# Modulation sums moved from TensorE products to VectorE inside three feed-forwards, with partition sums by ones and a reordered first stage

## The chip, the cores and the metric

The kernel runs on one core of one Trainium2 chip. The metric is the device time of one execution in microseconds (us). A core has a matrix engine (TensorE, PE in the profile; its weight loads are listed as PEld), three other compute engines that the profile calls DVE (VectorE), ACT (ScalarE) and POOL (GpSimd), and SP (SyncE), whose queue issues nearly all transfers here. Each engine works through its own queue in order; semaphores tie the queues together.

## What is computed

A two-layer block over 256 latent and 256 context tokens of width 1024, followed by a second two-layer block, all in float32. What matters here is the adaptive modulation of the first block:

```python
def adaln_modulation(cond, w_ada, b_ada):
    return jnp.split(jax.nn.silu(cond) @ w_ada + b_ada, N_MOD, axis=-1)   # N_MOD = 9

for layer in range(2):
    mods_lat = adaln_modulation(c, ada_w[layer], ada_b[layer])        # one vector of 1024
    mods_ctx = adaln_modulation(c_ctx, ada_w[layer], ada_b[layer])    # one vector of 1024
    x   = ffn_sublayer(x,   *mods_lat[0:3], ...)     # shift, scale, gate
    ctx = ffn_sublayer(ctx, *mods_ctx[0:3], ...)
    ... mixer with mods[3:6], then a feed-forward of the latent (and in layer 0 the context) with mods[6:9]
```

`ada_w[layer]` is 1024 x 9216, 36 MB; it is multiplied by only two vectors. In the code it is cut into 18 groups per layer (36 in all) of 512 output columns, 2 MB each. Two groups make one of the nine vectors, so groups 0 to 5 give shift, scale and gate of the first feed-forward, 6 to 11 those of the mixer and 12 to 17 those of the second feed-forward. The other operation that matters is the feed-forward, `(silu(x @ gate) * (x @ up)) @ down` with an inner width of 2816 = 22 chunks of 128.

## The kernel before

The program is written in the order of the model, and a planner in the language's framework lays out each engine's queue from that order and its own cost figures; what is emitted early can be put between instructions emitted later, and the queues are then fixed.

**Products.** Weights come as float32 into a raw tile (`wraw`, two buffers), ScalarE rounds them to `whi` (line 78) and VectorE subtracts to get `wlo` (line 81), four buffers each, one for half a chunk. `mm3` (lines 110 to 114) then makes three matmuls per block: high by high, high by low, low by high.

**Feed-forward.** `ffn` (line 1680) calls `gate_up`, which goes over 22 chunks `c`: load 1 MB, split it, and make 48 matmuls of 512 columns (gate and up, 8 row blocks, 3 matmuls each) into two PSUM banks; then ScalarE takes the silu into `h` (line 430) and VectorE multiplies (line 431). After it `rows_out` (line 434) multiplies by the down weights, 22 features of 24 matmuls.

**Modulation.** `ada_group(l, g)` (line 204) loads two tiles `fraw` of 1 MB (two buffers), makes 8 float32 products with the 32-column tile `sil` (silu of the two conditions) as the stationary operand, each on its own 32 columns of the array (line 215), copies the result to `far` (ScalarE, line 218), turns it by four transposes (line 221), sums the four quarters into `fm` (VectorE, line 223) and adds the bias. Each float32 product appears as two matmul instructions in the trace.

**Where the 36 groups stand.** Layer 0: groups 0 to 3 in `first_rows` (line 304), 4 to 9 between the chunks of the first feed-forward (every third chunk), 10 to 17 in the even mixer. Layer 1: 0 to 5 in the even mixer and its scan (`ada_next`), 6 to 9 in the third feed-forward, 10 to 17 ahead of the odd mixer's attention. In the even mixer VectorE also makes two convolutions: five taps in `conv5`, and 31 taps on four blocks in `conv31` (line 949), which the planner uses as filler from 493 us on.

**First stage.** `first_rows` computes groups 0 and 2, loads and turns the four token tiles `x`, computes group 1, modulates rows 0 to 3, loads gate and up chunk 0, computes group 3, loads chunk 1, and modulates rows 4 to 7. `gate_up` begins after all that.

Of the kernel before, what the change touches and what calls it, by code (L numbers as in the profile page):

```python
# [9 lines left out]
F32 = mybir.dt.float32  # L10
# [3 lines left out]
ALU = mybir.AluOpType  # L14
# [39 lines left out]
class Net:  # L54
    def __init__(self, tc, I, out, stop=None, dbg=None):
        self.tc, self.nc, self.I, self.out = tc, tc.nc, I, out
        self.stop, self.dbg = stop, dbg
        self.xtag = ("xtt", 2)
        self.mark = lambda label: None
        self.ahead = []  # L60
        self.pins = []
        self.norm = {}


# [138 lines left out]

    def ada_group(self, l, g):

        self.mark(f"ada{l}")
        nc = self.nc
        mod, half = divmod(g, 2)
        ps = self.pt(role="ada")
        w = self.I["ada_w"][l].rearrange("(k p) n -> p k n", p=128)  # L210
        for u in range(2):
            raw = self.fp.tile([128, 4, 512], F32, name="fraw", tag="fraw", bufs=self.FB)
            nc.sync.dma_start(raw, w[:, 4 * u:4 * u + 4, g * 512:(g + 1) * 512])
# [3 lines left out]
        r = self.fp.tile([128, 512], F32, name="far", tag="far", bufs=1)  # L217
        nc.scalar.copy(r, ps)
        p2 = self.pt([128, 4, 128], "ada")
        for j in range(4):  # L220
            nc.tensor.transpose(p2[:, j, :], r[:, 128 * j:128 * (j + 1)], self.ident)
        f = self.fm[l][:, mod, 4 * half:4 * half + 4, :]
        nc.vector.tensor_reduce(f, p2.rearrange("p j (q r) -> p j r q", q=4)[:, :, 0:2, :], axis=AX.X, op=ALU.add)
        b = self.adab[l][:, mod * 8 + 4 * half: mod * 8 + 4 * half + 4]
        nc.vector.tensor_add(f, f, b[:, :, None].to_broadcast([128, 4, 2]))

    def ada_next(self, n=1):

        for _ in range(min(n, len(self.fill))):
            self.ada_group(*self.fill.pop(0))  # L230
        self.mark("e_x")

# [71 lines left out]
    def first_rows(self, src, xh, xl):  # L304

        nc = self.nc
        xT = self.lp.tile([128, KC, 512], F32, name="xT")
        self.ada_group(0, 0)
        self.ada_group(0, 2)
        self.mark("xt0")  # L310
        for t in range(4):
            x = self.lp.tile([128, D], F32, name="x", tag="x", bufs=4)
            nc.sync.dma_start(x, src[t])
# [6 lines left out]
        self.ada_group(0, 1)  # L320
        self.mark("xt0")
        sc = self.cp.tile([128, KC, 2], F32, name="msc", tag="msc", bufs=2)
        bi = self.fm[0][:, 0]

        def modulate(k):
            if k % 4 == 0:
                nc.vector.tensor_scalar(sc[:, k:k + 4], self.fm[0][:, 1, k:k + 4], 1.0, None, op0=ALU.add)
            t = self.lp.tile([128, 512], F32, name="xtt", tag="xtt", bufs=2)
# [4 lines left out]
            self.lo(xl[:, k], t, xh[:, k])  # L333

        for k in range(4):
            modulate(k)
        self.ahead.append(self.gu_chunk(self.I["ffn_w_gu"][0, 0], 0))
        self.ada_group(0, 3)
        self.ahead.append(self.gu_chunk(self.I["ffn_w_gu"][0, 0], 1))
        self.mark("xt0")  # L340
        for k in range(4, KC):
            modulate(k)

    def xt_tiles(self, pool, T):
# [61 lines left out]

    def gate_up(self, wgu, xh, xl, T, h, fill=(), halves=()):
        nc = self.nc
        todo = []
        fill = list(fill)  # L410
        for c in range(NF):
            if fill and c >= 2 and c % 3 == 0:
                self.ada_group(*fill.pop(0))
                self.mark("gu")
            pieces = self.ahead.pop(0) if self.ahead else self.gu_chunk(wgu, c)
            ps = [self.pt([128, T]) for _ in range(2)]
            todo.append((c, pieces, ps))

            if c == 0 and T == 512:
# [9 lines left out]
            for cc, _, pp in todo:  # L429
                nc.scalar.activation(h(cc), pp[0], AF.Silu)  # L430
                nc.vector.tensor_mul(h(cc), h(cc), pp[1])
            todo = []

    def rows_out(self, w, nf, T, operand, done, keep=3, spare=None, banks=(0, 2, 4, 6), aside={}):
# [18 lines left out]
        for u in range(nf // 2):  # L453
# [3 lines left out]
            for q in range(2):  # L457
# [14 lines left out]
                if i < 0:  # L472
                    for t in range(nt):
                        prod(t, f)
                if f in aside:
                    aside[f]()
        for t in range(nt):
# [22 lines left out]
    def even(self, xh, xl):  # L500
# [148 lines left out]
        for h in range(4):  # L649
# [6 lines left out]
            tokmajor(c, khat[:, :, h, :])  # L656
            if h % 2:
                self.ada_next()
        rk = gd.tile([128, 16], F32, name="rk")
# [65 lines left out]
        for b2 in range(2):  # L725
            pv, pg = unit(2064 + 256 * b2), unit(2576 + 256 * b2)
            for j in range(2):
# [8 lines left out]
                pads.append(pad)  # L736
                self.ada_next()

# [3 lines left out]
        for h in range(4):  # L742
# [4 lines left out]
            sumsq(qT[:, h, :], h, pss)  # L747
            if h % 2:
                self.ada_next()
        rq = gd.tile([128, 16], F32, name="rq")  # L750
# [12 lines left out]
        for h in range(4):  # L763
# [6 lines left out]
            nc.sync.dma_start(kvd[:, :, 1, h, :].rearrange("t p c -> p t c"), vt)  # L770
            if h % 2:
                self.ada_next()

        self.mark("e_z")

        for h in range(4):
# [5 lines left out]
            nc.sync.dma_start(szd[h], c)  # L782
            if h % 2:
                self.ada_next()

# [3 lines left out]
    def even_scan(self, E):  # L789
# [187 lines left out]
        both(step(0, 3, False, False), step(1, 2, False, False))  # L977
        self.ada_next(20)
        merge(2)
# [10 lines left out]

    def odd(self, xh, xl, oh, ol, fill, aside):
        nc, tc, I = self.nc, self.tc, self.I
# [91 lines left out]
        self.roles(mm=[2, 3], tp=[0], sc=[4, 5], po=[1], ada=[6, 7])  # L1084
        for g in fill:
            self.ada_group(*g)
        self.mark("o_att")
        for h in range(8):
# [415 lines left out]
    def run(self):  # L1504
        nc, tc, I = self.nc, self.tc, self.I
        with ExitStack() as ctx:
# [24 lines left out]
            with tc.tile_pool(name="lp", bufs=1, reuse_waits="tile") as self.lp:  # L1531
                self.first_rows(raw, *xt)
            later()
            xt = self.ffn(0, 0, 512, xt, raw, src(0), lambda x: feed(0, (3, 4), 0, x), ada(0, 4, 10))
            if self.stop == "ffn00":
                return dump(0)
            with tc.tile_pool(name="yo", bufs=1, reuse_waits="tile") as self.yo:
                self.roles(mm=[2, 3], tp=[0, 1], ch=[4, 5], ada=[6], pss=[7])
                with tc.tile_pool(name="gd", bufs=1, reuse_waits="tile") as self.gd:
                    with tc.tile_pool(name="ip", bufs=1, reuse_waits="tile") as self.ip:  # L1540
                        self.fill = ada(0, 10, 18) + ada(1, 0, 6)
                        E = self.even(*xt)
# [10 lines left out]
            if self.stop == "mix0":  # L1553
                return dump(1)
            xt = self.ffn(0, 1, 512, xt, src(1), src(2), lambda x: feed(1, (0, 1), 2, x), cuts=((256, 512), (0, 256)))
            if self.stop == "x0c":
                return dump(2, 2)
            xt = self.ffn(1, 0, 512, xt, src(2), src(3), lambda x: feed(1, (3, 4), 3, x), ada(1, 6, 10))
            if self.stop == "x1a":
# [5 lines left out]
            with tc.tile_pool(name="oo", bufs=1, reuse_waits="tile") as oo:  # L1565
                ot = oo.tile([128, KC, 256], F32R, name="oh"), oo.tile([128, KC, 256], F32R, name="ol")
                with tc.tile_pool(name="od", bufs=1, reuse_waits="tile") as self.od:
                    self.roles(mm=[2, 3, 4, 5], tp=[0, 1], sc=[4, 5], po=[7], ada=[6])
                    self.odd(*xt, *ot, ada(1, 10, 18), lambda: self.memory_rows(0, self.od, *self.mem))
                xt = self.mix_out(1, I["attn_w_out"][0], 256, lambda f: (ot[0][:, f, :], ot[1][:, f, :]),  # L1570
# [108 lines left out]

    def ffn(self, l, i, T, xt, srcs, dsts, feed, fill=(), cuts=((0, 256), (256, 512))):  # L1680

# [3 lines left out]
        with tc.tile_pool(name="gp", bufs=1, reuse_waits="tile") as self.gp, \  # L1685
# [5 lines left out]
            h = lambda c: h0[:, c, :] if c < n0 else h1[:, c - n0, :]  # L1691
            self.roles(mm=[2, 3, 4, 5], tp=[0, 1], ada=[6, 7])
            self.mark(f"gu{l}{i}")
            self.gate_up(I["ffn_w_gu"][l, i], xt[0], xt[1], T, h, fill, cuts)
            self.mark(f"dn{l}{i}")
# [49 lines left out]
```

## Time and profile before

| | |
|---|---|
| median of 3 runs | 2547.15 us (2544.28 to 2547.5) |
| the profiled execution's own time | 2545.8 us |
| its span in the trace | 2544.0 us |
| mean granted TensorE clock | 0.992 of full speed |
| busy: PE, PEld | 2480.4, 2020.9 us |
| busy: DVE, ACT, POOL | 1417.3, 1053.4, 9.1 us |
| transfers | 395.78 MB, 156 GB/s in the mean |

The busy time of PE is modelled (a matmul's row lasts longer than the distance to the next one), so the rows below are mostly read by start times. A row of the timeline gives start, duration, engine, line, operation, output and inputs; in brackets, where shown, the idle time of the engine before it and what ended it.

### The profile page before, as it was taken

The page shows a single profiled execution, that of the slowest core. Times are in us where ns is not written, and L with a number is a line of the kernel's source. Part 1 is how long each engine was busy: PE and PEld are TensorE (multiplying, and loading weights), DVE is VectorE, ACT ScalarE, POOL GpSimd, SP SyncE. Part 2 cuts the span into 40 slices and gives each one's busy share as a digit, 9 for nine tenths or more (in the row PEclk, how much of TensorE's full clock was granted, in tenths as well). Part 3 has the DMA queues.
Part 4 walks back from the last instruction along what each step waited for, and adds up shares of the span by engine and source line. Part 5 has one row for each costly group of instructions (what it writes and reads, how often), then busy time and mean ns, then how long its engine had stood idle before and what let it go on. Part 6 is the DMA issues. An engine that isn't in the chain of part 4 may idle for free.

```text
span 2544.0 us, 33357 instructions
## 1 busy us (share of the span) xinstructions
PE 2480.4 (97%) x13192; PEld 2020.9 (79%) x13192; DVE 1417.3 (56%) x2699; ACT 1053.4 (41%) x1766; POOL 9.1 (0%) x42
## 2 busy tenths in 40 slices
PE   6999999999999999999999999999999999999998
PEld 4877887767888888888788887589978878888786
DVE  3322246699887422347322357665575766657755
ACT  2222234733334222224222325654455565556544
POOL 0000000000000000000000000000000000000000
PEclk8999999999999999999999999999999999999999
DMA  8545433476626333235453335768655335453354
GB/s 283 170 138 153 145 101 132 146 212 225 226 84 198 100 100 100 100 100 185 130 161 90 114 108 171 272 188 222 195 174 179 100 128 195 168 177 116 128 170 141
DMA packets 342634, 395.78 MB, mean 156 GB/s; under 512 B 19368, under 2 KB 236749, under 8 KB 342477
## 3 DMA queue, kind: packets, MB, share of 16 engines
q1 hardware_dynamic: 342477, 393.64, 49.0%
q8 instruction: 104, 1.70, 0.3%
q14 instruction: 53, 0.43, 0.1%
HBM read 377.06 MB, written 16.55 MB: 155 GB/s over the span
## 4 chain that ended last, share of the span: by engine, by line
PE 90%; DVE 5%; DMA 3%; ACT 1%; issue 1%; SPq 0%; DVEq 0%; ACTq 0%
PE b L112 26%; PE b L114 26%; PE b L113 26%; PE b L215 2%; DMA fraw<-in_ada_w 2%; PE b L1294 1%; PE b L287 1%; DVE wlo L81 1%; DMA wraw<-in_w_in 1%; DVE y L949 1%; PE b L1355 1%; PE b L1103 1%; PE b L1346 1%; PE b L822 0%; PE b L817 0%
## 5 line engine op out<-in xcount | busy, mean ns | idle before, releaser
L81 DVE TENSOR_TENSOR wlo<-wraw,whi 128x1024 fp32r<-128x1024 f32 (+2 forms) x499 | 600.5, 1207 | 692.2 <-ACT whi L78 691.1
L78 ACT CAST whi<-wraw 128x1024 fp32r<-128x1024 f32 (+2 forms) x499 | 514.0, 1039 | 500.5 <-PE b L113 289.9
L112 PE MATMUL b<-xh,whi 128*128 128x512 f32 (+1 forms) x1720 | 616.2, 359 | 4.0 <-ACT whi L78 2.7
L113 PE MATMUL b<-xl,whi 128*128 128x512 f32 (+1 forms) x1720 | 614.9, 358 | 0.0
L114 PE MATMUL b<-xh,wlo 128*128 128x512 f32 (+1 forms) x1720 | 612.5, 357 | 2.2 <-DVE wlo L81 2.1
L112 PEld LDWEIGHTS b<-xh,whi 128*128 128x128 f32 x1720 | 328.5, 191 | 63.8 <-issue 10.1
L113 PEld LDWEIGHTS b<-xl,whi 128*128 128x128 f32 x1720 | 328.8, 191 | 47.6 <-issue 4.2
L114 PEld LDWEIGHTS b<-xh,wlo 128*128 128x128 f32 x1720 | 328.1, 191 | 47.9 <-DVE wlo L81 3.7
L113 PE MATMUL b<-wlo,hh 128*128 128x512 f32 x652 | 254.6, 390 | 0.0
L112 PE MATMUL b<-whi,hh 128*128 128x512 f32 x652 | 254.4, 390 | 0.0
L114 PE MATMUL b<-whi,hl 128*128 128x512 f32 x652 | 254.3, 390 | 0.0
L430 ACT ACTIVATE h<-b 128x512 f32<-128x512 f32 (+1 forms) x88 | 47.9, 544 | 334.1 <-PE b L114 334.0
L112 PE MATMUL b<-whi,x 128*128 128x512 f32 (+1 forms) x448 | 172.3, 385 | 1.4 <-ACT xtt L294 1.4
L114 PE MATMUL b<-whi,x 128*128 128x512 f32 (+1 forms) x448 | 170.6, 381 | 0.0
L113 PE MATMUL b<-wlo,x 128*128 128x512 f32 (+1 forms) x448 | 170.5, 381 | 0.0
L112 PEld LDWEIGHTS b<-whi,hh 128*128 128x128 f32 x652 | 122.4, 188 | 26.2
L114 PEld LDWEIGHTS b<-whi,hl 128*128 128x128 f32 x652 | 122.4, 188 | 26.0
L113 PEld LDWEIGHTS b<-wlo,hh 128*128 128x128 f32 x652 | 122.5, 188 | 25.8
L81 DVE TENSOR_TENSOR hl<-h,hh 128x512 fp32r<-128x512 f32 (+1 forms) x81 | 50.2, 621 | 150.1 <-ACT hh L78 150.1
L78 ACT CAST hh<-h 128x512 fp32r<-128x512 f32 (+1 forms) x81 | 45.8, 567 | 195.6 <-PE b L113 189.5
L112 PEld LDWEIGHTS b<-whi,x 128*128 128x128 f32 x448 | 84.2, 188 | 18.0 <-issue 2.0
L215 PE MATMUL b<-fraw,sil 128*32 128x512 f32 x576 | 84.9, 644 | 12.8 <-DMA fraw<-in_ada_w 12.8
(477 smaller groups left out, 3232.0 us busy)
## 6 DMA issues: line engine op xcount, KB each, us to landing
wraw<-in_ffn_w_gu SPq DMA_DIRECT2D x176, 512.0 KB, 5.6
fraw<-in_ada_w SPq DMA_DIRECT2D x72, 1024.0 KB, 7.1
wraw<-in_w_in SPq DMA_DIRECT2D x64, 1024.0 KB, 5.1
wraw<-in_ffn_w_down SPq DMA_DIRECT2D x44, 1024.0 KB, 5.0
wraw<-in_even_w_in SPq DMA_DIRECT2D x12, 1024.0 KB, 6.6
wraw<-in_w_branch SPq DMA_DIRECT2D x12, 1024.0 KB, 4.9
xd<-x SPq DMA_DIRECT2D x16, 512.0 KB, 5.8
wraw<-in_w_mem_kv SPq DMA_DIRECT2D x8, 1024.0 KB
```

Of the source, the lines that this page charges most:

```text
L78: self.nc.scalar.copy(out, in_)
L81: return self.nc.vector.tensor_sub(out, in_, hi)
L112: mm(ps, ah, bh, start=start, stop=False)
L113: mm(ps, ah, bl, start=False, stop=False)
L114: mm(ps, al, bh, start=False, stop=stop)
L215: nc.tensor.matmul(ps[32 * q:32 * q + 32], self.sil[:, 4 * u + q, :], raw[:, q, :], start=(u == 0), stop=(u == 1))
L287: nc.tensor.transpose(ps[:, j, :], n[:, 128 * k:128 * (k + 1)], self.ident)
L430: nc.scalar.activation(h(cc), pp[0], AF.Silu)
L949: v.scalar_tensor_tensor(acc, pad[:, :, i:i + 256], w, acc, op0=ALU.mult, op1=ALU.add)
L1103: nc.tensor.matmul(po, vt[:, c, h // 4], pT[:, c], start=(c == 0), stop=(c == 3))
L1294: nc.tensor.matmul(ps, T[r, h // 2, 128 * t:128 * t + 128], K[r, 0:128 * (t + 1)], start=True, stop=True)
L1346: nc.tensor.transpose(p2[:, j, 128 * c:128 * c + 128], p[:, j, 128 * c:128 * c + 128], self.ident)
```

## The change

Groups 0 to 3 of layer 0 still use `ada_group`. The other 32 are made by a generator, `ada_sums`, that runs inside three feed-forwards: 12 groups (layer 0, 4 to 15) in the first, 12 (layer 0, 16 and 17; layer 1, 0 to 9) in the second, 8 (layer 1, 10 to 17) in the third. For each of the two conditions VectorE multiplies the eight 128 x 512 row blocks of a group by the condition's value on each partition and adds them up in a tile `facc`: 16 VectorE operations of 512 columns a group. Four matmuls with the first column of a constant tile of ones as the moving operand then sum over the 128 partitions, for each condition apart, and VectorE adds the bias. `gate_up` takes eight steps of the generator a chunk, `rows_out` four a feature, and the rest at its end. The even mixer, its scan and the odd mixer have no groups any more.

`first_rows` issues its loads in another order: group 0, the four token tiles, group 2, half of the weights of chunks 0 and 1, groups 1 and 3 (into six buffers of their own). It then makes the first halves of the products of chunks 0 and 1 as soon as rows 0 to 3 are modulated, groups 1 and 3 after them, and the rest of chunks 0 to 2; `gate_up` gets these three chunks ready made.

```diff
+    def ada_load(self, l, g, pool=None):
+        w = self.I["ada_w"][l].rearrange("(k p) n -> p k n", p=128)
+        out = []
+        for u in range(2):
...
+                raw = pool.tile([128, 4, 512], F32, name="araw", tag="araw", bufs=6)
+            self.nc.sync.dma_start(raw, w[:, 4 * u:4 * u + 4, g * 512:(g + 1) * 512])
...
-    def ada_next(self, n=1):
...
+    def ada_sums(self, groups):
+        def load(l, g, u):
+            raw = self.fp.tile([128, 4, 512], F32, name="fraw", tag="fraw", bufs=self.FB)
...
+        def total(l, g, s, acc):
+            if s == 0:
+                self.ada_ps = self.pt([128, 4, 2], "ada")
+            ps = self.ada_ps
+            mod, half = divmod(g, 2)
+            for j in range(4):
+                nc.tensor.matmul(ps[:, j, s:s + 1], acc[:, 128 * j:128 * (j + 1)], self.ones[:, 0:1],
+                                 start=True, stop=True)
+            if s:
...
+                nc.vector.tensor_add(self.fm[l][:, mod, 4 * half:4 * half + 4, :], ps,
+                                     b[:, :, None].to_broadcast([128, 4, 2]))
+        halves = [(l, g, u) for l, g in groups for u in range(2)]
...
+        raws = [load(*h) for h in halves[:2]]
+        acc = {}
+        for i, (l, g, u) in enumerate(halves):
+            raw = raws.pop(0)
+            for s in range(2):
+                if u == 0:
+                    acc[s] = self.lp.tile([128, 512], F32, name="facc", tag="facc", bufs=2)
+                for q in range(4):
+                    c = self.sil[:, 4 * u + q, s:s + 1]
+                    if u + q == 0:
+                        nc.vector.tensor_scalar(acc[s], raw[:, q], c, None, op0=ALU.mult)
+                    else:
+                        nc.vector.scalar_tensor_tensor(acc[s], raw[:, q], c, acc[s], op0=ALU.mult, op1=ALU.add)
+                    yield
+                if u:
+                    total(l, g, s, acc[s])
+            if i + 2 < len(halves):
+                raws.append(load(*halves[i + 2]))
...
     def first_rows(self, src, xh, xl):
-        self.ada_group(0, 0)
-        self.ada_group(0, 2)
...
+        loads = {0: self.ada_load(0, 0, lp)}
+        for t in range(4):
+            x = lp.tile([128, D], F32, name="x", tag="x", bufs=4)
+            nc.sync.dma_start(x, src[t])
+        loads[2] = self.ada_load(0, 2, lp)
...
+        raws = {(0, 0): piece(0, 0), (1, 0): piece(1, 0)}
+        self.ada_group(0, 0, loads.pop(0))
...
+        self.ada_group(0, 2, loads.pop(2))
+        loads[1] = self.ada_load(0, 1, lp)
+        loads[3] = self.ada_load(0, 3, lp)
...
         for k in range(4):
             modulate(k)
+        half(0, 0, acc[0])
+        raws[2, 0] = piece(2, 0)
+        half(1, 0, acc[1])
+        self.ada_group(0, 1, loads.pop(1))
+        self.ada_group(0, 3, loads.pop(3))
         for k in range(4, KC):
             modulate(k)
+        raws[0, 1] = piece(0, 1)
+        half(2, 0, acc[2])
+        raws[1, 1] = piece(1, 1)
+        for c in range(3):
+            if c == 1:
+                raws[2, 1] = piece(2, 1)
+            half(c, 1, acc[c])
+        return acc
...
     gate_up:   + self.ada_some(8)       # each chunk, after its load and split
     rows_out:  + self.ada_some(4)       # each of the first 17 features; at the end self.ada_some(200)
     even, even_scan:  - self.ada_next() # 14 groups
     odd:       - for g in fill: self.ada_group(*g)     # 8 groups
```

## Rows read from the trace of the kernel before

**Rows 1.** The profile page, busy time, share and instructions of each engine.

```profile
PE 2480.4 (97%) x13192; PEld 2020.9 (79%) x13192; DVE 1417.3 (56%) x2699; ACT 1053.4 (41%) x1766; POOL 9.1 (0%) x42
```

**Rows 2.** The chain that ended last: shares by engine, then by line.

```profile
PE 90%; DVE 5%; DMA 3%; ACT 1%; issue 1%; SPq 0%; DVEq 0%; ACTq 0%
PE b L112 26%; PE b L114 26%; PE b L113 26%; PE b L215 2%; DMA fraw<-in_ada_w 2%; PE b L1294 1%; PE b L287 1%; DVE wlo L81 1%; DMA wraw<-in_w_in 1%; DVE y L949 1%; PE b L1355 1%; PE b L1103 1%; PE b L1346 1%; PE b L822 0%; PE b L817 0%
```

**Rows 3.** Instructions grouped by line: count, busy us, mean ns, idle before and releasers.

```profile
L81 DVE TENSOR_TENSOR wlo<-wraw,whi 128x1024 fp32r<-128x1024 f32 (+2 forms) x499 | 600.5, 1207 | 692.2 <-ACT whi L78 691.1
...
L215 PE MATMUL b<-fraw,sil 128*32 128x512 f32 x576 | 84.9, 644 | 12.8 <-DMA fraw<-in_ada_w 12.8
...
L221 PE MATMUL b<-cst,far 128*128 128x128 f32 x144 | 24.2, 292 | 7.0 <-ACT far L218 6.9
```

**Rows 4.** Timeline of ScalarE, first feed-forward: chunks without and with a group.

```profile
103.60 0.60 ACT L430 ACTIVATE h<-b 128x512 f32<-128x512 f32 x1 [4.04 <-PE b L114]
106.14 1.05 ACT L78 CAST whi<-wraw 128x1024 fp32r<-128x1024 f32 x1 [1.94 <-PE b L113]
108.87 1.05 ACT L78 CAST whi<-wraw 128x1024 fp32r<-128x1024 f32 x1 [1.68 <-PE b L113]
114.48 0.60 ACT L430 ACTIVATE h<-b 128x512 f32<-128x512 f32 x1 [4.56 <-PE b L114]
...
127.94 0.60 ACT L430 ACTIVATE h<-b 128x512 f32<-128x512 f32 x1 [5.54 <-PE b L114]
```

**Rows 5.** Timeline of TensorE in the even mixer, at two products with ones.

```profile
462.10 0.48 PE L112 MATMUL b<-xh,whi 128*128 128x512 f32 x1
462.41 0.99 PE L556 MATMUL b<-cst,sq 128*128 128x1 f32 x8
...
463.58 0.40 PE L114 MATMUL b<-xh,wlo 128*128 128x512 f32 x1
...
476.58 0.39 PE L112 MATMUL b<-xh,whi 128*128 128x512 f32 x1
476.81 0.94 PE L556 MATMUL b<-cst,sq 128*128 128x1 f32 x8
...
477.94 0.40 PE L114 MATMUL b<-xh,wlo 128*128 128x512 f32 x1
```

**Rows 6.** Timeline of VectorE, multiply-adds of 512 columns in a row.

```profile
635.90 10.68 DVE L949 SCALAR_TENSOR_TENSOR y<-upad,vd,y 128x512 f32<-128x512 f32 x16
```

**Rows 7.** Busy times in stretches (columns: length, each engine, clock, DMA share, GB/s): feed-forwards.

```profile
828.00:1036.00 208.00, 208.00 (x919) 172.22 (x918) 66.01 (x64) 52.87 (x60) 0.00 (x0) 1.00 0.36 100
...
302.00:362.00 60.00, 60.00 (x267) 49.58 (x266) 21.76 (x24) 18.30 (x26) 0.00 (x0) 1.00 0.33 108
```

**Rows 8.** The same view, even mixer and scan.

```profile
433.00:493.00 60.00, 56.64 (x328) 42.87 (x327) 38.67 (x113) 42.23 (x76) 0.54 (x8) 0.97 0.50 163
493.00:577.00 84.00, 81.48 (x419) 56.81 (x418) 77.10 (x185) 32.86 (x55) 0.27 (x4) 0.98 0.68 202
577.00:645.00 68.00, 65.58 (x353) 47.96 (x350) 64.80 (x114) 26.57 (x38) 0.54 (x8) 0.97 0.68 230
645.00:692.00 47.00, 45.12 (x403) 38.45 (x403) 40.79 (x78) 18.01 (x46) 1.27 (x1) 1.00 0.78 272
692.00:745.00 53.00, 49.96 (x437) 45.99 (x437) 46.23 (x117) 16.31 (x42) 3.81 (x3) 1.00 0.14 42
```

**Rows 9.** The same view, attention of the odd mixer.

```profile
1592.00:1646.00 54.00, 51.95 (x291) 26.75 (x291) 33.28 (x119) 34.07 (x88) 0.00 (x0) 1.00 0.89 310
```

**Rows 10.** The same view, first stage, and the start of the second feed-forward.

```profile
34.00:51.00 17.00, 11.65 (x48) 7.12 (x49) 9.48 (x18) 9.07 (x14) 0.00 (x0) 0.51 1.11 344
794.00:809.00 15.00, 11.65 (x75) 10.98 (x74) 10.15 (x24) 8.14 (x21) 0.00 (x0) 0.77 0.84 245
```

**Rows 11.** Timeline of the first stage: first matmul of the feed-forward, third chunk done.

```profile
45.39 0.58 PE L112 MATMUL b<-xh,whi 128*128 128x256 f32 x1 [2.42 <-ACT whi L78]
...
79.27 0.60 ACT L430 ACTIVATE h<-b 128x512 f32<-128x512 f32 x1 [3.49 <-PE b L114]
```

More of the change, by code (lines that the diff above doesn't have):

```diff
@@ L59, in __init__ @@
         self.mark = lambda label: None
-        self.ahead = []
         self.pins = []
         self.norm = {}
+        self.sums = iter(())
     def roles(self, **banks):
@@ L209, in ada_group @@
         ps = self.pt(role="ada")
[L210 to L213, printed above, removed]
+        for u, raw in enumerate(raws or self.ada_load(l, g)):
             for q in range(4):
@@ L216, in ada_group @@
                                  start=(u == 0), stop=(u == 1))
-        r = self.fp.tile([128, 512], F32, name="far", tag="far", bufs=1)
+        r = self.lp.tile([128, 512], F32, name="far", tag="far", bufs=1)
         nc.scalar.copy(r, ps)
@@ L225, in ada_group, with ada_some @@
         nc.vector.tensor_add(f, f, b[:, :, None].to_broadcast([128, 4, 2]))
-    def ada_next(self, n=1):
-        for _ in range(min(n, len(self.fill))):
-            self.ada_group(*self.fill.pop(0))
-        self.mark("e_x")
+    def ada_sums(self, groups):
+        nc = self.nc
+        def load(l, g, u):
+            raw = self.fp.tile([128, 4, 512], F32, name="fraw", tag="fraw", bufs=self.FB)
+            w = self.I["ada_w"][l].rearrange("(k p) n -> p k n", p=128)
+            nc.sync.dma_start(raw, w[:, 4 * u:4 * u + 4, g * 512:(g + 1) * 512])
+            return raw
+        def total(l, g, s, acc):
[7 more added lines that the diff above has]
+            if s:
+                b = self.adab[l][:, mod * 8 + 4 * half: mod * 8 + 4 * half + 4]
+                nc.vector.tensor_add(self.fm[l][:, mod, 4 * half:4 * half + 4, :], ps,
+                                     b[:, :, None].to_broadcast([128, 4, 2]))
+        halves = [(l, g, u) for l, g in groups for u in range(2)]
+        if not halves:
+            return
+        raws = [load(*h) for h in halves[:2]]
[9 more added lines that the diff above has]
+                        nc.vector.tensor_scalar(acc[s], raw[:, q], c, None, op0=ALU.mult)
+                    else:
+                        nc.vector.scalar_tensor_tensor(acc[s], raw[:, q], c, acc[s], op0=ALU.mult, op1=ALU.add)
[4 more added lines that the diff above has]
+                raws.append(load(*halves[i + 2]))
+    def ada_some(self, n):
+        for _ in range(n):
+            next(self.sums, None)
     def gate_rows(self, l, mod, gw, streams):
@@ L333, in modulate, with half @@
             self.lo(xl[:, k], t, xh[:, k])
+        acc = [[self.pt(bank=2 * c + 2 + g) for g in range(2)] for c in range(2)]
+        def half(c, hf, ps):
+            wh, wl = self.split(raws.pop((c, hf)))
+            for k in range(4):
+                for g in range(2):
+                    self.mm3(ps[g], wh[:, k, g, :], wl[:, k, g, :], xh[:, 4 * hf + k], xl[:, 4 * hf + k],
+                             hf == 0 and k == 0, hf == 1 and k == 3)
         for k in range(4):
             modulate(k)
[L337 to L340, printed above, removed]
+        self.mark("gu00")
+        half(0, 0, acc[0])
[3 more added lines that the diff above has]
+        self.ada_group(0, 3, loads.pop(3))
+        acc.append([self.pt(bank=g) for g in range(2)])
         for k in range(4, KC):
             modulate(k)
+        raws[0, 1] = piece(0, 1)
[6 more added lines that the diff above has]
+        return acc
     def xt_tiles(self, pool, T):
@@ L405, in gu_chunk, with gate_up, out @@
         return [self.split(rv[:, 4 * q:4 * q + 4]) for q in range(2)]
-    def gate_up(self, wgu, xh, xl, T, h, fill=(), halves=()):
+    def gate_up(self, wgu, xh, xl, T, h, halves=(), ready=()):
         nc = self.nc
         todo = []
[L410 to L415, printed above, removed]
+        def out(c, ps):
+            nc.scalar.activation(h(c), ps[0], AF.Silu)
+            nc.vector.tensor_mul(h(c), h(c), ps[1])
+        for c, ps in enumerate(ready):
+            out(c, ps)
+        for c in range(len(ready), NF):
+            pieces = self.gu_chunk(wgu, c)
             ps = [self.pt([128, T]) for _ in range(2)]
             todo.append((c, pieces, ps))
+            self.ada_some(8)
             if c == 0 and T == 512:
@@ L988, in even_scan, with odd @@
         return o, y
-    def odd(self, xh, xl, oh, ol, fill, aside):
+    def odd(self, xh, xl, oh, ol, aside):
         nc, tc, I = self.nc, self.tc, self.I
```

61 lines of the change are left out of this document (30 added, 31 removed).

## Prediction

> **What bounds the kernel now.** I read the page's first part, the chain that ended last, the groups by line, and then busy times by stretch. TensorE (PE) is busy for 97% of the span [rows 1], and 90% of the chain is PE, nearly all of it the three matmul lines of `mm3` [rows 2]: the kernel is a queue of matmuls, and an edit is worth what it takes from or adds to that queue, stage by stage. The modulation has 2% of the chain as its products (line 215) and 2% as waits for its loads. In the feed-forwards VectorE is busy for 66.01 of 208 us [rows 7]; in the even mixer it is not idle at all: 77.10 of 84, 64.80 of 68, 40.79 of 47 and 46.23 of 53 us [rows 8]. So the change puts work where VectorE has room, and takes PE work out of a place where VectorE may be the next bound.
>
> **What a group costs PE now.** `h` of three successive chunks is started at 103.60, 114.48 and 127.94 [rows 4]: a chunk takes 10.88 us, one with a group 13.46. A group in a full PE queue costs 2.58 us.
>
> **What the new form costs PE.** The trace has the same operation, a product of 128 x 128 float32 weights with one column of ones (line 556). Four of them are eight matmul instructions. From the matmul ahead to the second one behind it takes 463.58 - 462.10 = 1.48 us at one place and 477.94 - 476.58 = 1.36 at the other [rows 5]; two ordinary matmuls take 2 x 10.88/48 = 0.45. So a sum costs 1.03 or 0.91 us, on average 0.97, and a group has two: 1.94 us. The change saves PE only 0.64 us a group; its worth lies in where the groups stand.
>
> On this the Trainium skill has a rule that reads otherwise (TensorE: Matmul & The Clock Gate, Back-to-back issue gap): an isolated matmul of 1 to 64 columns takes about 25 ns. By it a sum of eight would be 0.2 us and the whole kernel 49 us faster than by the rows, a rival below. The trace does not bear it out where the weights change with each matmul: both places above show about 0.1 us for each of the eight. The Trainium skill's LDWEIGHTS section of that page, 107 ns for 128 weight columns, agrees with these rows.
>
> **The sum, part by part.**
>
> *Feed-forwards.* They gain 32 groups in the new form, 62.1 us, and lose ten old ones (six in the first, four in the third), 25.8: **+36.3 us**, with bounds of 32.4 and 40.1 from 0.91 and 1.03. VectorE's part: sixteen multiply-adds in a row take 10.68 us, 0.667 each [rows 6], so eight a chunk are 5.3 us beside 66.01/19.1 = 3.5 us a chunk today [rows 7]: 8.8 of 11.85 us, 74%. Of the 192 steps of the first feed-forward 152 fall in its 19 chunks; the other 40, 26.7 us, fall in `rows_out`, where 21.8 of 60 us are taken [rows 7]. VectorE is hidden by PE in all of it. A chunk then moves 2.1 MB in 11.85 us, 177 GB/s, and 344 have been moved [rows 10]. The load of the tile after next waits on SP's queue until the eight steps of the present tile are through, and the next weights stand behind it; but rounding is released by PE, not by a load [rows 4], so the weights have time in hand.
>
> *Even mixer and scan.* It loses 14 groups: 2 before 493 us, 12 after. PE alone would gain 14 x 2.58 = 36 us. VectorE decides: from 493 to 745 it has 228.9 us of work in 252 [rows 8], less about 4 us that the groups themselves had. If the filler keeps it as full as in 577 to 645 (95%), 225/0.95 = 237 us, a gain of 15; at today's 91%, a gain of 5. Before 493 VectorE has 38.67 of 60 us, and PE's two groups with what they wait for give about 7. I take 15 + 7 = **-22 us**; bounds 10 (91%, and 5 before) and 38 (PE decides, with 2 us of waits).
>
> *Attention of the odd mixer.* Eight groups, 20.6 us of PE. In 1592 to 1646, with seven of them, PE has 51.95 of 54 us, VectorE 33.28 and ScalarE 34.07 [rows 9]. Without them some 36 us remain, in which both would be busy for five sixths; softmax passes between the two, so I take **-18 us**. Bounds: 12, if VectorE can be filled only to three quarters, and 25, if the waits for these loads (a part of the 12.8 us of line 215, [rows 3]) go too.
>
> *First stage.* Before the first product of chunk 0 at 45.39 [rows 11] stood four groups, the tokens and a chunk: 11 MB. Now it is two groups, the tokens and two half chunks: 7 MB. 4 MB (4.2 million bytes) less at the 344 GB/s of this stretch [rows 10] is 12.2 us, so it starts at 33.2. Three chunks are 32.6 us, groups 1 and 3, which now stand in between, 5.2; the clock, 0.51 of full here, cost 79.27 - 45.39 - 32.6 = 1.3 us, which I keep. That ends the third chunk at 72.3 in place of 79.27 [rows 11]: **-7 us**. Bounds: 0, if the loads, which stay the same in bytes, still set the end, and 10, if no cold time is left and the tokens' order saves a little more.
>
> Sum: -7 + 36.3 - 22 - 18 = -10.7 us on the profiled execution's 2545.8 us: **2535 us**. The median of the runs shown is 1.35 us above that execution, less than I can tell apart, and I add nothing. 0.2%, 5 us, is about what a measurement of this kernel can tell from no change.
>
> **Rivals.**
>
> *The mixers give back all of it.* If PE sets the pace in both: -7 + 36.3 - 38 - 25 = -33.7, 2512 us. For it: PE is nearly full there. Against: so is VectorE [rows 8].
>
> *The even mixer does not shrink, since VectorE is full.* Then 10 for 22: 2547 us, no change. For it: 64.80 of 68 us, and 87% even after the last group. Against: its 31-tap convolution is filler that can be put wherever there is room.
>
> *PE waits for VectorE in the feed-forwards (the other side).* The place is VectorE's in-order queue. `whi` of the next chunk is done at 107.19, that chunk starts at 114.48 [rows 4], and `wlo` takes 1.2 us [rows 3]: 6.1 us in hand, of which a block of eight takes 5.3. It decides from 0.8 us of further work ahead of a `wlo`, or when the planner puts a sum into PE's queue before its eighth step has ended; everything behind the sum then waits. At 0.4 us for each of 64 sums it is 26 us: 2561. For it: the small margin. Against: VectorE has 26% free, and two chunks of buffers soften it; `wlo` has only 1% of the chain now [rows 2].
>
> *The clock falls in the mixers.* Between 794 and 809, with PE idle for 3.4 us, the granted clock was 0.77 in the mean, a part at 1.2 GHz [rows 10]. Thinner attention and scan could do the same; 18 us of each at half the rate lose 9 and 9: 2553. Against: 0.97 and 1.00 there now, and PE stays over 85% busy.
>
> *A sum of ones is cheap.* At 0.2 us for 0.97 the 64 sums save 49 us: 2486. The two places in rows 5 speak against it.
>
> **How the numbers follow.** Chances: the forecast, at 2523 to 2545, 0.50; the mixers give all, 0.12; the even mixer does not shrink, 0.18; PE waits for VectorE, 0.12; the clock, 0.04; cheap ones, 0.04. The range of 2511 to 2556 leaves out the cheap ones, the far part of the first rival, and most of the wait for VectorE, about 2 in 10. Faster by over 0.2% (below 2542): 0.42 of the forecast's 0.50, 0.12 and 0.04, 0.58. Within 0.2%: 0.08 and two thirds of the even mixer's, 0.20. Slower: the rest, 0.22.
>
> **What the profile after would show.** Cadence of `h`: 10.88 plus about 0.97 a chunk in the feed-forwards where groups are summed; eight one-column matmuls in 0.81 to 0.85 us; VectorE's busy share there near 74%; no idle time of PE ended by `facc`. The even mixer and scan shorter by 22 us with VectorE at 95%; attention shorter by 18; the third chunk done near 72 us. The forecast is wrong if PE's waits name `facc` or `wlo` in the feed-forwards, if the stretch from 433 to 745 keeps its length, or if a sum costs much less than 0.9 us.

## The result, and the profile after

The change made the kernel slower, by 0.6%. The median went from 2547.32 us to 2564.08 us (2560.34 to 2564.88 in four runs), a ratio of 1.0061 with a 95% interval of 1.0048 to 1.0074. I had forecast 2535 us, with a range that ended at 2556.

Ahead of the places, the page of the kernel after, to be read against [rows 1, 2]: busy time of the engines, and the chain that ended last by engine.

```profile
PE 2461.6 (96%) x12968; PEld 2059.3 (80%) x12968; DVE 1747.9 (68%) x3179; ACT 1034.1 (40%) x1734; POOL 10.6 (0%) x42
...
PE 84%; DVE 8%; ACT 3%; DMA 2%; issue 1%; POOL 0%; SPq 0%; POOLq 0%; DVEq 0%; ACTq 0%
```

PE has 18.8 us less to do and VectorE 330.6 us more. The span is 2562.8 us for 2544.0: PE's work went down, its waiting went up. VectorE's share of the chain rose from 5% to 8%, though I had put all its new work behind PE. The mean granted clock fell from 0.992 to 0.983.

The table says where. Each entry is the start of the same instruction in that kernel's trace less its start in the trace of before, in us; the step from one line to the next is what a stage won or lost. The last three columns are experiments told below.

| up to | after | none left over | more left over | first stage alone |
|---|---|---|---|---|
| `h` of the third chunk | -11.5 | -11.8 | -13.2 | -10.6 |
| last `h` of the first feed-forward | -11.0 | -7.6 | -18.4 | -14.2 |
| transposes of the even mixer's first products | +14.1 | -9.6 | +32.5 | -16.1 |
| last `yp` product, the even mixer's end | +4.1 | -20.8 | +21.9 | -14.2 |
| last `h` of the second feed-forward | +18.6 | -1.7 | +31.5 | -14.0 |
| first `h` of the third | +23.2 | -1.6 | +72.7 | -14.0 |
| first product of the odd mixer | +28.1 | +6.6 | +77.0 | -14.0 |
| last `p` transposes of its attention | +19.0 | -2.7 | +67.7 | -14.3 |
| last output products | +18.6 | -3.9 | +66.3 | -11.5 |

The first stage won more than I had said. What the first feed-forward lost, it lost between its last `h` and the transposes of the even mixer's first products, called its tail below: 25.1 us, in a stretch to which I had given nothing.

First the part that went as told. These are ScalarE's starts of `h` in three chunks of the first feed-forward (start, duration), and PE's sum with ones in the chunk after them:

```profile
101.14 0.60 ACT L505 ACTIVATE h<-b 128x512 f32<-128x512 f32 x1 [5.51 <-PE b L114]
112.97 0.60 ACT L505 ACTIVATE h<-b 128x512 f32<-128x512 f32 x1 [5.57 <-PE b L114]
124.80 0.60 ACT L505 ACTIVATE h<-b 128x512 f32<-128x512 f32 x1 [5.57 <-PE b L114]
```

```profile
130.04 0.95 PE L254 MATMUL b<-cst,facc 128*128 128x1 f32 x8
```

The cadence is 11.83 us where a chunk alone takes 10.88 [rows 4]: a sum costs 0.95 us (I had 0.97), and PE does not wait there for VectorE's eight steps.

Now the lost stretch. VectorE's timeline, at the last steps ahead of the down projection and in its tail:

```profile
284.94 0.48 DVE L274 TENSOR_SCALAR facc<-fraw,sil 128x512 f32<-128x512 f32 x1
...
286.47 5.47 DVE L276 SCALAR_TENSOR_TENSOR facc<-fraw,sil,facc 128x512 f32<-128x512 f32 x7
...
415.87 0.69 DVE L475 SCALAR_TENSOR_TENSOR x<-x,b 128x512 f32<-128x512 f32 x1
...
418.60 0.17 DVE L258 TENSOR_TENSOR fm<-b,va 128x8 f32<-128x8 f32 x1 [1.31 <-PE b L254]
418.68 0.87 DVE L274 TENSOR_SCALAR facc<-fraw,sil 128x512 f32<-128x512 f32 x2
419.47 9.36 DVE L276 SCALAR_TENSOR_TENSOR facc<-fraw,sil,facc 128x512 f32<-128x512 f32 x14
...
435.24 0.88 DVE L274 TENSOR_SCALAR facc<-fraw,sil 128x512 f32<-128x512 f32 x2
436.03 9.36 DVE L276 SCALAR_TENSOR_TENSOR facc<-fraw,sil,facc 128x512 f32<-128x512 f32 x14
445.30 0.81 DVE L482 TENSOR_SCALAR x<-x,mv,rs 128x1024 f32<-128x1024 f32 x1
```

PE's sums and its transposes of the normalized tokens in the same stretch:

```profile
416.61 1.95 PE L254 MATMUL b<-cst,facc 128*128 128x1 f32 x16
431.62 3.49 PE L254 MATMUL b<-cst,facc 128*128 128x1 f32 x16
444.87 3.54 PE L254 MATMUL b<-cst,facc 128*128 128x1 f32 x16 [5.49 <-DVE facc L276]
...
454.26 1.94 PE L342 MATMUL b<-cst,x 128*128 128x128 f32 x8 [4.04 <-DVE x L482]
```

And the busy times by stretch (length, then PE, PEld, VectorE, ScalarE, POOL; the granted clock stands behind POOL):

```profile
301.00:362.00 61.00, 61.00 (x271) 50.52 (x270) 23.77 (x26) 20.31 (x27) 0.00 (x0) 1.00 0.34 113
...
425.00:440.00 15.00, 8.56 (x38) 8.26 (x38) 12.54 (x23) 0.00 (x0) 0.00 (x0) 0.66 0.63 206
440.00:465.00 25.00, 14.49 (x70) 13.52 (x71) 13.60 (x36) 10.94 (x23) 0.00 (x0) 0.59 0.11 43
```

Between 301 and 362 VectorE is busy for only 23.77 of 61 us, and not one of the leftover steps runs there, though this is where I had put them. Eight of the 40 had run by 292; the pair of sums that closes their group starts only at 416.61. The code says why: `rows_out` for 512 columns takes all eight PSUM banks (0, 2, 4, 6, each with its neighbour) for its accumulators, and a sum needs bank 6 or 7. Until token tile 3's accumulator is read, no sum can be made; until the sum is made, both `facc` buffers are taken; so the other 32 steps wait as well. The trace fits this: VectorE's read of the accumulator at line 475 ends at 416.56, the sums start at 416.61, and the profile names that read as what they waited for. When the bank comes free they run as two blocks of 10.2 us, in order, on the engine that is to normalize the last two token tiles, which the even mixer needs first. PE meanwhile has too little to do: 23 of 40 us busy, and at 0.66 and 0.59 the granted clock is for the greater part at 1.2 GHz, after idle time of PE. The same sixteen sum instructions take 3.49 us there for 1.95.

PE's waits in the whole trace (total, times, longest) show it less plainly, because the wait is spread over several names. The longest of each of these three lies in this stretch, and two of them, `facc` and `wlo`, are the names by which I had said that a wrong forecast would be known:

```profile
PE b L114 <- DVE wlo L81: 6.6, 2, 6.1
PE b L254 <- DVE facc L276: 6.3, 2, 5.5
...
PE b L342 <- DVE x L482: 5.3, 4, 4.0
```

### The profile page after: what moved, and what is told of

It is laid out like the page before. It is cut to its first block, busy times and chain, and to the rows that moved or that the text cites. A ratio compares the mean times of both kernels' runs of the same rounds, so it can differ in the third digit from the quotient of the medians.

```text
span 2562.8 us, 33431 instructions
## 1 busy us (share of the span) xinstructions
PE 2461.6 (96%) x12968; PEld 2059.3 (80%) x12968; DVE 1747.9 (68%) x3179; ACT 1034.1 (40%) x1734; POOL 10.6 (0%) x42
## 4 chain that ended last, share of the span: by engine, by line
PE 84%; DVE 8%; ACT 3%; DMA 2%; issue 1%; POOL 0%; SPq 0%; POOLq 0%; DVEq 0%; ACTq 0%
PE b L112 24%; PE b L113 24%; PE b L114 24%; PE b L254 2%; PE b L1379 1%; DVE wlo L81 1%; DVE y L1038 1%; PE b L342 1%; DMA araw<-in_ada_w 1%; DVE facc L276 1%; ACT xtt L351 1%; DMA wraw<-in_w_in 1%; ACT whi L78 1%; PE b L1188 1%; PE b L1440 1%
## 5 line engine op out<-in xcount | busy, mean ns | idle before, releaser
L276 DVE SCALAR_TENSOR_TENSOR facc<-fraw,sil,facc 128x512 f32<-128x512 f32 x448 | 326.4, 749 | 9.7 <-DMA fraw<-in_ada_w 1.6
```

Of the source, the lines that this page charges most:

```text
L276: nc.vector.scalar_tensor_tensor(acc[s], raw[:, q], c, acc[s], op0=ALU.mult, op1=ALU.add)
```

## The experiments

The theory (A) was that the leftover steps do the harm. The rivals were that VectorE is too full in the feed-forwards in any case (B), and that the gain is lost in the even mixer to VectorE's convolution (C).

**None left over.** Eleven steps a chunk in place of eight, so that all are done within `gate_up`.

```diff
-            self.ada_some(8)
+            self.ada_some(11)
```

> The changed kernel with eleven multiply-adds for each feed-forward chunk in place of eight, so that none is left over for the down projections (40 were left in the first feed-forward, 16 in the second). Theory A, the leftovers do the harm, since they can't get a PSUM bank while the down projection holds all eight and then stand in VectorE's queue amid the layer norms: the stretch from the last h of the first feed-forward to the first products of the even mixer loses its 25 us, the second feed-forward's 4.6 us go too, and the kernel comes to 2564 - 20 to 30 = 2534 to 2544 us, no slower than before. Theory B, VectorE is too full in the feed-forwards in any case: eleven a chunk are 7.3 us beside 3.5 of 11.8 us, PE now waits for wlo within the chunks, and the time stays at 2560 or rises. Theory C, the even mixer bound by VectorE's convolution is what the gain is lost to: the time moves by less than 5 us, since the mixer is not touched.

Measured: 2545.28 us for 2548.76 beside it, ratio 0.999 (0.9981 to 0.9999). One number took 19 us off the change. The tail of the first feed-forward costs -2.0 us in place of +25.1, that of the second +0.1 in place of +4.6. Theory A holds, a little below the 20 to 30 us that it had said. Theory B has a small part: up to their last `h` the three feed-forwards now take 31.4 us more than before, with eight steps 19.9. Nine more sums stand in them, which at 0.95 us make 8.6; some 3 us are left for B.

**More left over.** Six steps a chunk: 78 and 60 are left in place of 40 and 16.

```diff
-            self.ada_some(8)
+            self.ada_some(6)
```

> The changed kernel with six multiply-adds a chunk in place of eight: 78 are left over in the first feed-forward in place of 40, and 60 in the second in place of 16. Theory A: each leftover step is 0.667 us of VectorE in the tail's queue, and some sums at a cold clock go with it; 38 and 44 more steps are 25 and 29 us more of VectorE, so 2564 + 30 to 55 = 2594 to 2619 us. Theory B (VectorE too full within the chunks): fewer steps a chunk help, 2555 to 2564. Theory C: no change, 2560 to 2568.

Measured: 2612.29 us, ratio 1.0256 (1.0241 to 1.027). PE's waits now name the sums:

```profile
PE b L254 <- DVE facc L276: 41.9, 7, 10.0
PE b L342 <- DVE x L482: 10.8, 4, 5.3
```

The tail of the first feed-forward costs -2.0, +25.1 and +50.9 us with 0, 40 and 78 steps left over. In the second it is +0.1, +4.6 and +41.1 with 0, 16 and 60. Against none left over that is 0.68 us a step in the first tail, and 0.28 and 0.68 in the second; VectorE's own time is 0.667 [rows 6]. That the two agree is in part chance: in the first feed-forward eight of the 40 steps and 14 of the 78 run by 292 us, and the 32 and 64 that wait cost 0.85 and 0.83 us each, more than their own length. PE's work at the lower clock comes on top. Sixteen are for the greater part absorbed.

**The first stage alone.** The kernel before with `first_rows` and `ada_load` of the change; the other groups are as before.

```diff
-            xt = self.ffn(0, 0, 512, xt, raw, src(0), lambda x: feed(0, (3, 4), 0, x), ada(0, 4, 10))
+            xt = self.ffn(0, 0, 512, xt, raw, src(0), lambda x: feed(0, (3, 4), 0, x), ada(0, 4, 10), ready=ready)
```

> The kernel before with the new first stage alone: groups 0 to 3 in the new order of loads and three chunks ready, all other groups as before. The trace of the whole change had the third chunk's h 11.5 us earlier, and nothing behind it depends on the stage: 2547 - 11 = 2536 us, if what is won at the start is kept to the end. If the earlier start only meets a later wait (a rival: the loads of the next weights set the pace, and the lead is lost within the first feed-forward), 2543 to 2547.

Measured: 2530.78 us, ratio 0.993 (0.9916 to 0.9943). The lead is kept, and grows from 10.6 us at the third chunk to 14.2 at the last. This kernel is faster than both before and after, and of those in this study that leave nothing out none is measurably faster.

**The sums alone.** The change with the old first stage, and no steps in the first three chunks, so that 40 are left over again.

```diff
-            self.ada_some(8)
+            if c >= 3 or T != 512 or not self.first:
+                self.ada_some(8)
```

> The change without its first stage: groups 0 to 3 and their loads as before, the 32 groups as VectorE sums, none in the first three chunks so that 40 steps are left over as in the change. If the parts add up, the change's 2564 + 11 = 2575 us: the sums by themselves cost some 28 us against the kernel before. If the new first stage is what crowds the first feed-forward (a rival: it brings the loads and the sums closer together), 2560 to 2566.

Measured: 2575.78 us, ratio 1.0112 (1.0098 to 1.0126): 27 us over before. The parts alone, -18 and +27, make +9 where the whole is +16.8; they add up to within 8 us. Where the 8 us come from was not separated.

**The convolution cut, all 14 groups away.** The kernel with none left over, with only 11 of the convolution's 31 taps: it leaves out 80 steps of VectorE, so it serves to find the bound and does not compute the block.

```diff
-            for i in range(31):
+            for i in range(11):
```

> The changed kernel with eleven multiply-adds a chunk, as in the run before, and with 11 of the 31 taps of the even mixer's convolution; 20 taps of each of the four channel blocks are left out, 80 steps of VectorE or some 53 us at 0.667 each, and nothing of TensorE's. Theory: the even mixer and scan without their 14 groups are bound by VectorE, and the convolution that ends last is what PE waits for (10.3 us at lv, after 40 us in which it runs thin). Then the stretch from the first even product to the last yp product, 11 us shorter than before with all taps, comes near what 14 groups cost PE, 30 to 36 us, and the kernel is 2545 - 15 to 25 = 2520 to 2530 us. Rival: PE's own chain of dependent small products sets the scan's end and VectorE is only filler; then 2540 to 2545.

**The same cut in the kernel before.** The same edit.

> The kernel before with the same 80 convolution steps left out and nothing else changed: what the taps alone are worth where the 14 groups still fill PE. PE has 353 of 367 us in this stretch before, so at most 14 us can be gained and a few are likely: 2547 - 0 to 8 = 2539 to 2547 us. If VectorE already bound the mixer before (the rival), 20 us or more: below 2527.

Measured: 2528.19 us (ratio 0.9919, 0.9903 to 0.9934) and 2543.43 us (0.9984, 0.9974 to 0.9993). The even mixer, from its first products to the last `yp` product, is 11.2 us shorter than before without the 14 groups, 5.0 us shorter without the taps, and 32.9 us shorter without both. Two gains that come to 16 us one by one and to 33 together mean that VectorE takes over as the bound as soon as PE has less to do. With all taps, PE's scan is done 41.7 us early by its last `dm` products (the scan's last step), and then waits for the convolution's normalization. The kernel with none left over, PE's timeline:

```profile
705.00 0.66 PE L1048 MATMUL b<-cst,y 128*128 128x128 f32 x4 [2.09 <-DVE y L1038]
715.95 3.65 PE L1059 MATMUL b<-cst,lv 128*128 128x128 f32 x16 [10.30 <-DVE lv L1056]
```

and its busy times in that place:

```profile
705.00:740.00 35.00, 24.38 (x114) 20.18 (x115) 30.85 (x71) 16.22 (x38) 1.06 (x1) 0.80 0.57 195
```

**Ten groups as sums.** The first stage, and only the ten groups that already stood in the first and third feed-forward in the new form, six steps a chunk.

```diff
-            if fill and c >= 2 and c % 3 == 0:
-                self.ada_group(*fill.pop(0))
...
+            self.ada_some(6)
```

> The new first stage, and only those ten groups as VectorE sums that already stood in the first and third feed-forward (six steps a chunk, none left over); the other 22 groups as before, in the even mixer, the scan and the odd attention. By the sums' cadence of 0.95 us a group costs 1.90 of PE in place of 2.58: ten save 6.8 us on the 2531 of the first stage alone, 2524 us. Rival: the old groups cost nothing like 2.58 us beyond what PE would wait anyway, or VectorE's steps hinder the rounding: 2531 or more.

Measured: 2532.01 us, ratio 0.9937 (0.9922 to 0.9951). The forecast of 2524 missed. Between the third and the last `h` the first feed-forward took 214.8 us for 218.6 with the first stage alone, the third 222.5 for 225.4 between its second `h` and its last: the sums save 3.9 and 2.8 us, as told. Elsewhere it came back: the third chunk ends 2.3 us later, and the start of the second feed-forward loses some 3.6 us to a wait that the other kernel does not have, with the clock down behind it. Its PE timeline and busy times there:

```profile
789.27 1.94 PE L349 MATMUL b<-cst,x 128*128 128x128 f32 x8 [5.71 <-DVE x L489]
```

```profile
785.00:800.00 15.00, 9.99 (x61) 9.62 (x62) 7.67 (x15) 6.23 (x16) 0.00 (x0) 0.66 0.83 263
```

The first stage alone had 12.13 us of PE and a clock of 0.77 in the same stretch. Why VectorE was late with `x` there I did not separate. These are differences between two single executions: the one of the first stage alone that was traced took 2534.53 us, 3.8 above its median.

**The odd mixer's groups.** As the run before, with its eight groups moved to the third feed-forward, nine steps a chunk.

```diff
-            self.ada_some(6)
+            self.ada_some(9)
...
-            xt = self.ffn(1, 0, 512, xt, src(2), src(3), lambda x: feed(1, (3, 4), 3, x), ada(1, 6, 10))
+            xt = self.ffn(1, 0, 512, xt, src(2), src(3), lambda x: feed(1, (3, 4), 3, x), ada(1, 6, 18))
...
-                    self.odd(*xt, *ot, ada(1, 10, 18), lambda: self.memory_rows(0, self.od, *self.mem))
+                    self.odd(*xt, *ot, [], lambda: self.memory_rows(0, self.od, *self.mem))
```

> As the run before, with the odd mixer's eight groups too moved to the third feed-forward as VectorE sums (nine steps a chunk, none left over). Eight groups cost 8 x 1.90 = 15.2 us there. My forecast of the prediction, 18 us won in the attention, would give 2524 + 15.2 - 18 = 2521 us. What the trace of the whole change shows, 7.6 us won, gives 2524 + 15.2 - 7.6 = 2532 us: a loss of 8.

Measured: 2534.18 us, ratio 0.9945 (0.9932 to 0.9957). Against the run of ten, the third feed-forward's `gate_up` costs 14.2 us more and the odd mixer 10.4 less, up to the last transposes of its attention. The 18 us are not there. Busy times where the attention begins, in the kernel before:

```profile
1592.00:1605.00 13.00, 11.33 (x67) 4.63 (x70) 12.62 (x53) 9.33 (x29) 0.00 (x0) 1.00 0.89 305
```

and in this run, with PE's timeline there:

```profile
1592.00:1605.00 13.00, 7.90 (x29) 4.38 (x28) 11.76 (x47) 8.40 (x26) 0.00 (x0) 0.95 0.38 128
1605.00:1620.00 15.00, 15.00 (x63) 9.59 (x62) 10.72 (x30) 10.14 (x24) 0.00 (x0) 0.93 0.19 65
```

```profile
1595.82 0.63 PE L1182 MATMUL b<-cst,qo 128*128 128x128 f32 x4 [1.60 <-ACT sq L1126]
1598.17 1.12 PE L1199 MATMUL b<-kT,qT 128*128 128x512 f32 x2 [0.65 <-ACT sq L1126]
```

Without the groups PE is busy for 7.90 of the first 13 us, with them for 11.33, while VectorE (11.76) and ScalarE work on the last queries and the first heads; later it is full again. Groups had stood in that gap.

**Six of the even mixer's groups, taken from its late places.** They go to the first feed-forward, eleven steps a chunk there; eight stay, and fill the first eight places.

```diff
-            self.ada_some(6)
+            self.ada_some(11 if self.first else 6)
...
-            xt = self.ffn(0, 0, 512, xt, raw, src(0), lambda x: feed(0, (3, 4), 0, x), ada(0, 4, 10), ready=ready)
+            xt = self.ffn(0, 0, 512, xt, raw, src(0), lambda x: feed(0, (3, 4), 0, x), ada(0, 4, 16), ready=ready)
...
-                        self.fill = ada(0, 10, 18) + ada(1, 0, 6)
+                        self.fill = ada(0, 16, 18) + ada(1, 0, 6)
```

> The new first stage and the ten groups as sums, as in the run of ten, and six of the even mixer's 14 groups moved to the first feed-forward as sums too (eleven steps a chunk, none left over); eight stay in the even mixer, eight in the odd attention. Six groups cost 6 x 1.90 = 11.4 us in the feed-forward. By the theory that VectorE's convolution binds the even mixer only once PE has lost enough (with all 14 gone its end was 32 us early for PE but 11 for the products behind the convolution), the first six come off PE at about 2.3 us each: 13 to 15 us, so 2532 + 11.4 - 14 = 2529 us, and the PE work of the mixer and scan is done 14 us earlier with little wait at lv. If VectorE binds from the first group on, the six win 6 x 0.8 = 5 us and the kernel is 2538.

Measured: 2540.25 us, ratio 0.9961 (0.9946 to 0.9975). That is near the second case, but the trace does not show a mixer 5 us shorter: in it the even mixer is 4.0 us longer than before, though PE had some 15 us less to do. The execution that was traced took 2545.43 us, 5.2 above the median, the longest of six (from 2534.57), so the 4.0 us are uncertain by about as much. Busy times in three slices, first of the run of ten, with all 14 groups:

```profile
577.00:617.00 40.00, 40.00 (x212) 28.79 (x211) 39.25 (x68) 16.72 (x24) 0.27 (x4) 1.00 0.68 230
617.00:657.00 40.00, 38.54 (x330) 33.76 (x329) 37.14 (x62) 14.81 (x34) 0.00 (x0) 1.00 0.70 237
657.00:697.00 40.00, 37.70 (x310) 32.30 (x310) 32.77 (x76) 12.26 (x28) 2.55 (x2) 1.00 0.42 153
```

and of this run, 8 us later on its clock:

```profile
585.00:625.00 40.00, 34.95 (x161) 28.43 (x160) 39.71 (x65) 14.10 (x20) 0.27 (x4) 0.92 0.36 112
625.00:665.00 40.00, 36.75 (x295) 33.19 (x293) 35.47 (x56) 12.68 (x28) 0.00 (x0) 0.95 0.38 120
665.00:705.00 40.00, 34.46 (x277) 32.71 (x277) 33.63 (x74) 13.01 (x30) 2.54 (x2) 0.96 0.37 125
```

VectorE does the same amount in the same time. PE has gaps where the groups stood, and some of the time runs at the lower clock.

**The same six from the early places.** The eight that stay stand at the last eight places.

```diff
             tokmajor(c, khat[:, :, h, :])
-            if h % 2:
-                self.ada_next()
...
                 pads.append(pad)
-                self.ada_next()
```

> As the run before (first stage, ten sums, six more groups of the even mixer as sums in the first feed-forward), but the eight groups that stay in the even mixer stand at its last eight places (q, v, z and the scan) and the first six places (k and the gated part) stay empty; in the run before it was the other way round, and taking six groups from the late places shortened the mixer by nothing. Theory D, a group costs its 2.3 to 2.6 us only where PE is full (the first 110 us of the mixer, 39.9 of 40 us a slice), and is nearly free where PE waits for VectorE and for the chain of small products: now the six come off at full price, 14 us, and the first feed-forward's 11.4 us are paid back: 2540 - 14 to 18 = 2522 to 2526 us. Theory E, VectorE's total in the mixer sets its length wherever the groups stand: 2536 to 2542.

Measured: 2538.28 us, ratio 0.9966 (0.9953 to 0.9978). The even mixer is 3.9 us shorter than before, not 14. Theory D is refuted, and the time is what E said. In the two traces the place moves the mixer by 8 us, but the medians differ by only 2, so that is not shown to be more than the spread.

**Six late groups away, and the taps cut.** As two runs before, with only 11 of the 31 taps, so again a kernel that leaves out a part of the block.

```diff
-            for i in range(31):
+            for i in range(11):
```

> The run with six groups taken from the late places of the even mixer, with 11 of the 31 taps of its convolution; 80 steps of VectorE, 53 us, are left out. With all taps the stretch from the first even product to the last yp product was 4 us longer than before although PE had 15 us less to do. If VectorE's work is what fills the gap, the stretch becomes 12 to 20 us shorter than before, 2520 to 2527 us in all. If it is the chain of small dependent products with nothing to fill PE and the clock that falls with it (0.87 to 0.96 in five of eight slices), the stretch is at most 5 to 8 us shorter, as the kernel before was with these taps left out, and the time is 2530 to 2536.

Measured: 2525.47 us, ratio 0.9917 (0.9904 to 0.9931). The even mixer is 16.3 us shorter than before. With VectorE relieved, six groups are worth 16.3 - 5.0 = 11.3 us and 14 are worth 32.9 - 5.0 = 27.9: 1.9 and 2.0 us each. With all taps, six are worth between -4.0 and +3.9 in the two traces, and 14 are worth 11.

## Why the prediction was wrong

**The step that failed** is in "Feed-forwards": "the other 40, 26.7 us, fall in `rows_out`", and "VectorE is hidden by PE in all of it". I compared busy times, found 38 us of VectorE free, and did not ask what else a step needs: a sum needs a PSUM bank, a further step a `facc` buffer that the sum gives back, and `rows_out` holds every bank. The work came after `rows_out`, on the path: 25.1 and 4.6 us. The two dose experiments show that the leftovers are the cause. That a bank and a buffer are what holds them is read from the code, from the order in the trace and from the read at line 475 that the first waiting sums were released by; more `facc` buffers, or a bank kept free, were not tried, so that part stays argued.

**Rivals.** "PE waits for VectorE in the feed-forwards" named the right pair of engines, the side and nearly the time (2561 us), but put the wait into the chunks, where it did not happen with eight steps; that its time came near the measured one is luck, since the mixers' shortfall is in the measured time too. The clock rival was a consequence: it fell where PE had been made idle.

**Feed-forwards, the products.** A sum at 0.95 us for 0.97 was right. By the Trainium skill's 25 ns for an isolated product of few columns (TensorE: Matmul & The Clock Gate, Back-to-back issue gap) it would, as an estimate, have been 0.2. The trace does not agree: the cadence shows 0.12 us for each of the eight instructions. That section of the Trainium skill says that its figure leaves out the loading of weights. Here a weight load stands with each of the sum's instructions (L254 has as many of PEld as of PE). VectorE's share there was the 74% forecast, 140.17 of 189.40 us. Up to their last `h`, the three feed-forwards cost 0.5 + 14.5 + 4.9 = 19.9 us by the table, less than my +36.3: 55 of the 64 sums stood there, and the starts of the first and the second ran shorter than before.

**Even mixer and scan.** Forecast -22, measured -10.0 after and -11.2 with none left over. I took the convolution for filler "that can be put wherever there is room". There was no room: VectorE's work in the stretch stayed what it was (299.30 us before, 296.29 after), PE's shrank. Nor did VectorE get fuller, as the forecast needed: it was busy for 91% of the stretch, not 95%. The lower end of my bounds, 10, which was also the rival "the even mixer does not shrink", was the truth.

**Attention of the odd mixer.** Forecast -18, measured -9.1 over the odd mixer. My stretch began at 1592, behind the projection's last product, and from there 11.2 us were won, just outside the bound of 12: PE has gaps in the first heads that the groups had filled. The other 2.1 were lost ahead of it, in the projection, where the first of the eight groups had stood at 1563 us.

**First stage.** Forecast -7, measured -11.5 at the third chunk and some -18 in the medians of the first stage alone. Products start at 27.84, not at 33.2, 17.6 us earlier than before where I had 12.2 for the bytes that went. The loads also ran at a higher rate for a part of the time, 415 GB/s between 10 and 15 us for 236 before; what else moved the start was not separated.

By size: the tails took 29.7 us, the even mixer 12.0 and the odd one 8.9 more than I had said; the products in the feed-forwards gave back 16.4 and the first stage 4.5. That is 29.7 us, for the 29.3 between -10.7 and +18.6; the 0.4 were won behind the attention. The mixers' shortfall of 20.9 and the 20.9 given back happen to cancel: that the tails alone make up the whole miss is chance.

## What to carry to other kernels

Free time on an engine is not room for work: list what each moved instruction takes besides the engine (a PSUM bank, a buffer that another engine returns), and who holds it in the stretch to which it is to go. Work that fills the gaps of another engine's chain has a price far below its duration, so before taking it out, cut the suspected bound by itself and see whether the gain appears. And time the parts of a change apart: here one of two was worth 0.7% by itself, and the other hid it.

## What the runs showed of the hardware

Taking work away from PE lowered its clock in places: in the traced execution of the even mixer without six groups the granted clock was 0.92, 0.95 and 0.96 in three slices of 40 us in which it is 1.00 with them. Sixteen one-column products, 1.95 us at a granted clock of 1.00, took 3.49 and 3.54 us at 0.50 in the tail, so a delay that idles PE is paid again in the work behind it.
